# Three small moves in a transformer kernel: conv weights halved on GpSimd, bias copies moved into the feed-forward part, selector and factor tiles of the head norms widened to 128 partitions

## The chip, the cores and the metric

One core of a Trainium2 chip runs the whole kernel. A core has TensorE (PE, with its weight loads in rows of their own, PEld), VectorE (DVE), ScalarE (ACT), GpSimd (POOL) and the queues that start transfers (SP's, ACT's and POOL's). The metric is the device time in microseconds; several runs are given, and one more execution was profiled.

## The reference

Two blocks on 256 tokens of width 1024, in fp32. The first is a hybrid layer (dilated attention beside a state-space scan, then a gated feed-forward part). The second has two layers that work on a context stream `c` and an image stream `x` of 256 tokens each. In each: a modulated norm and a feed-forward part, a mixing part, and a second feed-forward part. The mixing part of the first of these layers normalizes each head of its queries and keys; that of the second has latent attention, and a neighbourhood attention with a relative bias. Cut to what the change touches:

```python
def causal_depthwise_conv(x, w, bias):        # block 1: four taps a channel, then silu
...
def rms_norm(x, gain=None):                   # used per head: x is (B, S, heads, 64)
    y = xf * lax.rsqrt(jnp.mean(xf * xf, axis=-1, keepdims=True) + EPS)
...
    aq = apply_rope2d(rms_norm(aq.reshape(B, S, A_HEADS, HEAD_DIM), a_q_norm), *rope)
    ak = apply_rope2d(rms_norm(ak.reshape(B, S, A_KV_HEADS, HEAD_DIM), a_k_norm), *rope)
...
        bias = rpb_f[:, dr_idx[None, :, None], dc_idx[:, None, :]]   # neighbourhood attention
        s = jnp.einsum('bqhd,bjkhd->bhqjk', q_row, k_band).astype(jnp.float32) * scale + bias
```

## The kernel before

**Products.** Activations lie transposed, features on partitions and tokens in the free dimension. Each fp32 product is made of three matmuls in the type fp32r: `wh` by the high part of the activations (L139), `wh` by their low part (L140), `wl` by the high part (L141). A weight slab of 128 x 1024 (512 KB) is loaded by SP's queue into one of five `wraw` buffers (L113); ACT makes `wh` of it by a cast (L120), DVE makes `wl` by a subtraction (L121). A slab feeds 24 matmuls of 256 or 512 columns. In the first block and on `x` alone the moving side has 256 columns; where `c` and `x` are taken side by side it has 512.

**Order.** `K.run` issues units (one column of 128 outputs each) and pieces of other work between them: `weave` spreads a list of steps over a list of units, and `later` puts a step off until the next product has been issued, so that PE has work while other engines prepare. A scheduler then orders the instructions of each engine by priority.

**Head norms.** `HeadNorm` belongs to the mixing parts `mix_ab` and `mix_cd`. For each block of 128 outputs (two heads of 64, or a head's 64 with 32 rotary rows) ACT copies and squares the product (`add`). A matmul with a block of ones gives the heads' sums of squares with tokens on partitions (L1047, two columns). DVE turns them into 1/rms. Two transposes (L1056) bring these factors back to one row per head, and `K.split` writes their high part into rows 0 to n-1 and their low part into rows 32 to 32+n-1 of a tile `rh` (`self.r`, one of a ring of four), the other rows being zero. Then, for each block, L1071 multiplies a selector `sel` by `rh`, which spreads each head's factor over the partitions of that head in PSUM, and DVE multiplies the block by it (L1073, or L1077 to L1081 with rotary tables). L1071 stands between matmuls of the products, one at a time or in pairs.

**Start of block 1.** `start` halves the taps and biases of the convolution (`cw`, L908), which are part of the constants `cols` that a DMA brings. DVE also sums squares for the first norm (`acc`, L322; PE sums them over partitions at L345), and copies the attention's bias rows out of PSUM (L507, after L506 on PE). POOL's queue writes these rows out (L508) and loads them back as bias tiles (L527).

**Neighbourhood bias.** `rpb` is a DRAM tile with 64 copies of the bias (8 heads x 889), so that `mix_cd` can read it with a skew (`load_bias`, on SP's queue, with an addition on POOL at L1615). `bias_rows` makes 8 steps of 8 copies each, from DRAM to DRAM on POOL's queue (L1643). `block2` puts them among the 40 background pieces of the feed-forward part of its first layer; since they wait for nothing, the scheduler sets them early.

Of the kernel before, what the change touches and what calls it, by code (L numbers as in the profile page):

```python
# [8 lines left out]
F32 = mybir.dt.float32  # L9
F32R = mybir.dt.float32r  # L10
AF = mybir.ActivationFunctionType
ALU = mybir.AluOpType
# [4 lines left out]
T = 256  # L17
# [446 lines left out]
def block1(K, start_mod):  # L464
    nc, tc, A = K.nc, K.tc, K.A
# [14 lines left out]
    cw = xpool.tile([128, 128], F32, name="cw")[:, :120]  # L480
    K.gap(xpool, 320)
    K.gap(xpool, 352)
    at, _ = COLS["conv_w"]
# [421 lines left out]
    sctx, qctx, yctx = ExitStack(), ExitStack(), ExitStack()  # L905

    def start():
        nc.vector.tensor_scalar(cw, K.cols[:, at:at + 120], 0.5, None, op0=ALU.mult)  # L908

    def heads_done():  # L910
        hctx.close()
# [28 lines left out]

    scan0 = scan(0)
    items = weave(qkv_units(0), [bias_row(0), start, bias_row(1), lambda: load_bias(0), bias_row(2)], 3, 2)
    items += weave(qkv_units(1) + [dt_unit] + b_units, attention(0) + [lambda: load_bias(1)])
    items += weave(qkv_units(2) + c_units + x_units(0), attention(1) + [lambda: load_bias(2)])
# [21 lines left out]
    fctx = ExitStack()  # L966
    K.gap(K.pool(fctx, "gap1", 1), 192)
    hid_p = K.pool(fctx, "b1h", 14)

    def c_square(b):  # L970
        return lambda: K.square_add("c", K.X["c"][:, b], b == 0)

    steps = K.pieces(16) + [c_square(b) for b in range(KB)]
# [114 lines left out]
def head_selectors(K, pool, width, rows, n):  # L1088

    nc, A = K.nc, K.A  # L1090
    at, n2 = COLS[f"sum{width}"]
    sums = K.cols[:rows, at:at + n2]
    raw = K.raw_p.tile([128, 1024], F32, name="wraw")
    sel = pool.tile([48, n * 128], F32R, name=f"sel{width}")
    nc.scalar.dma_start(raw[:48, :n * 128], A[f"sel{width}"])
    nc.vector.tensor_copy(sel, raw[:48, :n * 128])
    return sums, sel


def stacked(K, pool):  # L1100

    zero = K.t1("zero")
    K.nc.vector.memset(zero, 0.0)
    ring = []
    for i in range(4):
        ring.append(pool.tile([48, T], F32R, name=f"rh{i}"))
        K.nc.scalar.copy(ring[i], zero[:48])
    return ring


# [63 lines left out]
def out_proj(K, src, layer, streams, done, steps=()):  # L1174
    def evac(m):
        return lambda s, p: K.residual(s, m, p, K.mod(layer, s, 5)(m), True)

    K.run(weave([K.lin(src, m, K.acts, evac(m)) for m in range(KB)], steps), streams, done=done)


def mix_ab(K, streams):
# [14 lines left out]
    rctx = ExitStack()  # L1196
    rp = K.pool(rctx, "abr", 1)
    s64, sel64 = head_selectors(K, rp, 64, 128, 5)
    ring = stacked(K, rp)
    cos, sin = K.t1("cos"), K.t1("sin")  # L1200
    nc.scalar.dma_start(cos, A["rope_cos"])
# [209 lines left out]
def mix_cd(K, streams):  # L1411
# [28 lines left out]
    tctx = ExitStack()  # L1440
    tp = K.pool(tctx, "cdt", 1)
    s64, sel64 = head_selectors(K, tp, 64, 128, 5)
    s96, sel96 = head_selectors(K, tp, 96, 96, 4)
    ring = stacked(K, tp)

    rank = {("q", "x"): 6, ("k", "x"): 2, ("k", "c"): 2}
# [189 lines left out]
    ctx.close()  # L1636


def bias_rows(K):

    K.rpb = K.dram.tile([64, 8, 7 * 127], F32, name="rpb")
    rows = K.A["rpb"][:, 4:11].rearrange("h r c -> h (r c)").unsqueeze(0).to_broadcast([8, 8, 7 * 127])
    return [lambda i=i: K.nc.gpsimd.dma_start(K.rpb[8 * i:8 * i + 8], rows) for i in range(8)]  # L1643


def block2(K, layers=(0, 1)):
    nc, A = K.nc, K.A
    for layer in layers:
        both = ["c", "x"]

        def norms(i, layer=layer):
            return lambda s: K.norm_stream(s, K.mod(layer, s, i + 1), K.mod(layer, s, i))

        steps = K.pieces(40)
        if layer == 0:
            steps[10:10] = bias_rows(K)
        fctx = ExitStack()
        hid_p = K.pool(fctx, "h1", 14)
        K.ffn(A[f"f1g{layer}"], A[f"f1u{layer}"], [A[f"f1d{layer}{i}"] for i in range(3)], both,
              lambda s, m: K.mod(layer, s, 2)(m), hid_p, steps, norms(3))  # L1660
        fctx.close()
        K.dbg(f"d_xf{layer}", K.X["x"])
        K.dbg(f"d_cf{layer}", K.X["c"])
        if layer == 0:
            mix_ab(K, both)
            out_proj(K, A["ab_out"], 0, both, norms(6))
            tail = both
        else:
            while K.bg:
                K.background()  # L1670
            K.mctx.close()
            mix_cd(K, both)
            out_proj(K, A["cd_out"], 1, ["x"], norms(6))
            tail = ["x"]
        K.dbg(f"d_xm{layer}", K.X["x"])
        K.dbg(f"d_cm{layer}", K.X["c"])
        fctx = ExitStack()
        if layer == 1:
            K.gap(K.pool(fctx, "gap2", 1), 192)
        hid_p = K.pool(fctx, "h2", 14)  # L1680

        def done(s):
            K.norm_stream(s, K.mod(1, s, 1), K.mod(1, s, 0))

        def after(s, m):
            if layer == 1:
                nc.sync.dma_start(A["out"][:, m], K.X["x"][:, m])

        K.ffn(A[f"f2g{layer}"], A[f"f2u{layer}"], [A[f"f2d{layer}{i}"] for i in range(3)], tail,
              lambda s, m: K.mod(layer, s, 8)(m), hid_p, K.pieces(40 if layer == 0 else 0),  # L1690
              done if layer == 0 else None, after)
        fctx.close()
        K.dbg(f"d_x2{layer}", K.X["x"])
# [62 lines left out]
def constants():  # L1756
    import numpy as np
    f = np.float32
    c = {}
    i = np.arange(128)  # L1760
    c["ident"] = np.eye(128, dtype=f)
    c["tri"] = (i[:, None] <= i[None, :]).astype(f)
    for g, d in ((1, 4), (2, 16)):
        seg = T // d
        ok = (i[:, None] // seg == i[None, :] // seg) & (i[:, None] >= i[None, :])
        c[f"mask{g}"] = np.where(ok, 0.0, NEG).astype(f)

    def bucket(dist):
        dist = np.asarray(dist)
        big = 16 + (np.log(np.maximum(dist, 1).astype(f) / f(16)) / f(math.log(2048 / 16)) * f(16)).astype(np.int32)  # L1770
        return np.where(dist < 16, dist, np.minimum(big, 31))

    oh = np.zeros((33, 896), f)
    for g, (c0, n, off, d) in enumerate(((0, 383, 255, 1), (384, 255, 127, 4), (640, 255, 127, 16))):
        u = np.arange(n)
        oh[np.where((off - u >= 0) & (off - u <= 128), bucket(np.clip(off - u, 0, 128) * d), 32), c0 + u] = 1.0
    c["onehot"] = oh
    sel = np.zeros((8, 512), f)
    for h in range(8):
        sel[h, h * 64:h * 64 + 64] = 1.0  # L1780
    c["sel"] = sel
    for name, rows, n in (("sel64", [64, 64], 5), ("sel96", [64, 32], 4)):
        sel = np.zeros((48, n, 128), f)
        for b in range(n):
            at = 0
            for e, r in enumerate(rows[:2]):
                sel[[2 * b + e, 32 + 2 * b + e], b, at:at + r] = 1.0
                at += r
        c[name] = sel.reshape(48, n * 128)
    t = np.arange(T)  # L1790

    def rope(dim):
        nf = dim // 4
        inv = (f(10000.0) ** (-np.arange(nf, dtype=f) / f(nf))).astype(f)
        ang = np.concatenate([(t // 64).astype(f)[:, None] * inv, (t % 64).astype(f)[:, None] * inv], axis=-1)
        cos, sin = np.cos(ang.astype(np.float64)).astype(f), np.sin(ang.astype(np.float64)).astype(f)
        full = lambda a, sign: np.stack([sign * a.reshape(T, 2, nf), a.reshape(T, 2, nf)], axis=2).reshape(T, dim).T
        return full(cos, 1), full(sin, -1)

    cos, sin = rope(64)  # L1800
    c["rope_cos"], c["rope_sin"] = np.tile(cos, (2, 1)), np.tile(sin, (2, 1))
    cos, sin = rope(32)
    c["mla_cos"] = np.concatenate([np.ones((64, T), f), cos])
    c["mla_sin"] = np.concatenate([np.zeros((64, T), f), sin])
    q, k = i[:, None], i[None, :]
    c["amask"] = np.stack([np.where(k + 128 - q <= 128, 0.0, NEG), np.where(q + 128 - k <= 128, 0.0, NEG)], 1).astype(f)
    cq = np.tile(np.arange(64), 2)[:, None]
    ck = np.tile(np.arange(64), 4)[None, :]
    start = np.clip(cq - 8, 0, 48)
    c["dmask"] = np.where((ck >= start) & (ck < start + 16), 0.0, NEG).astype(f)  # L1810
    return {k: np.ascontiguousarray(v, dtype=f) for k, v in c.items()}


def prepare(inp):
    import numpy as np
    f = np.float32
    I = {k: np.asarray(v) for k, v in inp.items()}
    out = constants()
    feat = lambda a: np.ascontiguousarray(a.reshape(T, KB, 128).transpose(2, 1, 0))
    out["x"], out["ctx"] = feat(I["x"][0]), feat(I["ctx_2"][0])  # L1820
# [101 lines left out]
```

## Time and profile before

| | |
|---|---|
| Time of three runs | 2482.21, 2473.56, 2483.57 us, median 2482.21 |
| Time of the profiled execution | 2473.19 us |
| Its span, first to last instruction | 2471.4 us |
| PE busy | 2415.3 us, 98% |
| PEld (weight loads, beside PE) | 2101.6 us, 85% |
| DVE, ACT, POOL busy | 1642.8, 1064.7, 34.3 us |
| Mean granted TensorE clock | 0.985 |

PE is busy nearly all the time in every stage but the first microseconds. "Busy" says only that PE had a matmul in it: how fast these follow each other is read from their starts. The profiled execution took 1.8 us more than its span, and 9.0 us less than the median of the three runs.

### The profile page before, as it was taken

The page shows a single profiled execution, that of the slowest core. Times are in us where ns is not written, and L with a number is a line of the kernel's source. Part 1 is how long each engine was busy: PE and PEld are TensorE (multiplying, and loading weights), DVE is VectorE, ACT ScalarE, POOL GpSimd, SP SyncE. Part 2 cuts the span into 40 slices and gives each one's busy share as a digit, 9 for nine tenths or more (in the row PEclk, how much of TensorE's full clock was granted, in tenths as well). Part 3 has the DMA queues.
Part 4 walks back from the last instruction along what each step waited for, and adds up shares of the span by engine and source line. Part 5 has one row for each costly group of instructions (what it writes and reads, how often), then busy time and mean ns, then how long its engine had stood idle before and what let it go on. Part 6 is the DMA issues. An engine that isn't in the chain of part 4 may idle for free.

```text
span 2471.4 us, 38395 instructions
## 1 busy us (share of the span) xinstructions
PE 2415.3 (98%) x15104; PEld 2101.6 (85%) x15104; DVE 1642.8 (66%) x3016; ACT 1064.7 (43%) x1934; POOL 34.3 (1%) x56
## 2 busy tenths in 40 slices
PE   7999999999999999999999999999999999999999
PEld 6998999999988888886498888888888888876999
DVE  5767787787865666778757666656555555667655
ACT  4566565535632222535743222243222234555443
POOL 3000000000000000000000000000000000000000
PEclk9999899999999999999899999999999999999999
DMA  9455455676454554341014555534555422233554
GB/s 271 153 154 157 134 175 174 212 251 225 148 177 136 170 173 144 112 139 52 1 52 154 165 159 162 165 108 142 180 166 171 150 87 84 100 97 86 169 195 133
DMA packets 113157, 363.38 MB, mean 147 GB/s; under 512 B 21186, under 2 KB 23562, under 8 KB 112976
## 3 DMA queue, kind: packets, MB, share of 16 engines
q1 hardware_dynamic: 109232, 352.58, 45.1%
q0 software_dynamic: 2176, 5.09, 0.9%
q10 hardware_dynamic: 1568, 3.25, 0.4%
q8 instruction: 119, 1.95, 0.3%
q14 instruction: 62, 0.51, 0.1%
HBM read 359.33 MB, written 3.36 MB: 147 GB/s over the span
## 4 chain that ended last, share of the span: by engine, by line
PE 70%; DVE 3%; ACT 2%; issue 1%; DMA 0%; ACTq 0%; DVEq 0%
PE pm L139 20%; PE pm L140 20%; PE pm L141 20%; PE pt L1140 1%; PE pa L1047 1%; PE pm L1339 1%; PE pt L1071 1%; PE pa L1592 1%; DVE wl L121 1%; PE pm L1600 1%; PE pa L1355 1%; PE pm L1279 1%; PE pa L1316 0%; PE pm L1622 0%; PE pm L1165 0%
## 5 line engine op out<-in xcount | busy, mean ns | idle before, releaser
L139 PE MATMUL pm<-ah,wh 128*128 128x256 f32 (+2 forms) x3096 | 1002.9, 326 | 13.1 <-ACT ah L370 10.7
L140 PE MATMUL pm<-al,wh 128*128 128x256 f32 (+2 forms) x3096 | 997.4, 323 | 1.1 <-DVE al L371 1.0
L141 PE MATMUL pm<-ah,wl 128*128 128x256 f32 (+2 forms) x3096 | 996.1, 322 | 0.0
L120 ACT CAST wh<-wraw 128x1024 fp32r<-128x1024 f32 (+4 forms) x535 | 541.0, 1014 | 946.0 <-PE pm L140 750.3
L121 DVE TENSOR_TENSOR wl<-wraw,wh 128x1024 fp32r<-128x1024 f32 (+4 forms) x535 | 627.5, 1176 | 228.3 <-ACT wh L120 225.8
L139 PEld LDWEIGHTS pm<-ah,wh 128*128 128x128 f32 (+1 forms) x3096 | 590.1, 192 | 67.8 <-ACT ah L370 12.3
L140 PEld LDWEIGHTS pm<-al,wh 128*128 128x128 f32 (+1 forms) x3096 | 591.9, 191 | 49.0 <-issue 2.7
L141 PEld LDWEIGHTS pm<-ah,wl 128*128 128x128 f32 (+1 forms) x3096 | 592.2, 191 | 46.6 <-issue 2.3
L140 PE MATMUL pm<-hl,wh 128*128 128x512 f32 (+1 forms) x934 | 312.6, 335 | 0.0
L139 PE MATMUL pm<-hh,wh 128*128 128x512 f32 (+1 forms) x934 | 312.1, 334 | 0.0
L141 PE MATMUL pm<-hh,wl 128*128 128x512 f32 (+1 forms) x934 | 312.1, 334 | 0.0
L1001 DVE SCALAR_TENSOR_TENSOR junk<-wraw,cactc 128x1024 f32<-128x1024 f32 x112 | 137.2, 1225 | 183.1 <-DMA wraw<-w_mod 183.0
L1001 DVE SCALAR_TENSOR_TENSOR junk<-wraw,cactx 128x1024 f32<-128x1024 f32 x144 | 176.1, 1223 | 48.8 <-DMA wraw<-w_mod 46.2
L139 PEld LDWEIGHTS pm<-hh,wh 128*128 128x128 f32 x934 | 175.7, 188 | 18.7
L140 PEld LDWEIGHTS pm<-hl,wh 128*128 128x128 f32 x934 | 175.7, 188 | 18.6
L141 PEld LDWEIGHTS pm<-hh,wl 128*128 128x128 f32 x934 | 175.8, 188 | 18.4
L125 ACT CAST hh<-g 128x512 fp32r<-128x512 f32 (+1 forms) x113 | 59.1, 525 | 228.4 <-DVE g L428 228.4
L428 DVE TENSOR_TENSOR g<-g,pm 128x512 f32<-128x512 f32 (+1 forms) x113 | 64.0, 567 | 55.6 <-PE pm L141 54.1
L126 DVE TENSOR_TENSOR hl<-g,hh 128x512 fp32r<-128x512 f32 (+1 forms) x113 | 63.9, 567 | 0.3
L458 DVE SCALAR_TENSOR_TENSOR xc<-pm,mcol0c,xc 128x256 f32<-128x256 f32 x56 | 26.9, 481 | 53.5 <-PE pm L141 53.3
L424 ACT ACTIVATE g<-pm 128x512 f32<-128x512 f32 (+1 forms) x116 | 55.9, 486 | 2.0 <-PE pm L141 2.0
L1140 PEld LDWEIGHTS pt<-ident,e 128*128 128x128 f32 x272 | 30.7, 145 | 22.0 <-issue 18.6
(425 smaller groups left out, 2260.0 us busy)
## 6 DMA issues: line engine op xcount, KB each, us to landing
wraw<-w_mod SPq DMA_DIRECT2D x144, 512.0 KB, 4.0
wraw<-f1g SPq DMA_DIRECT2D x44, 512.0 KB, 3.9
wraw<-f1u SPq DMA_DIRECT2D x44, 512.0 KB, 4.2
wraw<-f2g SPq DMA_DIRECT2D x44, 512.0 KB, 3.6
wraw<-f2u SPq DMA_DIRECT2D x44, 512.0 KB, 3.6
wraw<-f1d SPq DMA_DIRECT2D x32, 512.0 KB, 3.9
wraw<-f2d SPq DMA_DIRECT2D x32, 512.0 KB, 3.6
wraw<-w_xbc SPq DMA_DIRECT2D x24, 512.0 KB, 3.7
```

The source lines that it names most:

```text
L120: nc.scalar.copy(h[:, :f], raw[:, :f])
L121: nc.vector.tensor_tensor(lo[:, :f], raw[:, :f], h[:, :f].bitcast(F32), op=ALU.subtract)
L125: self.nc.scalar.copy(h, src)
L126: self.nc.vector.tensor_tensor(lo, src, h.bitcast(F32), op=ALU.subtract)
L139: nc.tensor.matmul(out, h[:, c], ah, start=first, stop=False)
L140: nc.tensor.matmul(out, h[:, c], al, start=False, stop=False)
L141: nc.tensor.matmul(out, lo[:, c], ah, start=False, stop=last)
L424: nc.scalar.activation(half(g["g"], s), p, AF.Silu)
L428: nc.vector.tensor_tensor(t, t, p, op=ALU.mult)
L458: self.nc.vector.scalar_tensor_tensor(x, p, gate, x, op0=ALU.mult, op1=ALU.add)
L1001: nc.vector.scalar_tensor_tensor(junk, raw, 1.0, K.cact[s], op0=ALU.mult, op1=ALU.mult, accum_out=K.mcol[layer, s][:, j:j + 1])
L1140: nc.tensor.transpose(p[:, j * 128:(j + 1) * 128], b, K.ident)
```

## The change

Three parts. `cw` is halved on POOL in place of DVE (L908). `sel` and the four tiles of the ring have 128 partitions in place of 48 (the selector's constant, its load, its cast and the ring's zeroing with them), so L1071 contracts over 128 rows, of which the new ones are zero. And `bias_rows` first loads the 8 x 889 bias into an SBUF tile `rpbrow` of the feed-forward part's pool `h1`, then writes the 64 copies from there; the pool is opened ahead of it.

```diff
@@ mix1: start
-        nc.vector.tensor_scalar(cw, K.cols[:, at:at + 120], 0.5, None, op0=ALU.mult)
+        nc.gpsimd.tensor_scalar(cw, K.cols[:, at:at + 120], 0.5, None, op0=ALU.mult)
@@ head_selectors
-    sel = pool.tile([48, n * 128], F32R, name=f"sel{width}")
-    nc.scalar.dma_start(raw[:48, :n * 128], A[f"sel{width}"])
-    nc.vector.tensor_copy(sel, raw[:48, :n * 128])
+    sel = pool.tile([128, n * 128], F32R, name=f"sel{width}")
+    nc.scalar.dma_start(raw[:, :n * 128], A[f"sel{width}"])
+    nc.vector.tensor_copy(sel, raw[:, :n * 128])
@@ stacked
-        ring.append(pool.tile([48, T], F32R, name=f"rh{i}"))
-        K.nc.scalar.copy(ring[i], zero[:48])
+        ring.append(pool.tile([128, T], F32R, name=f"rh{i}"))
+        K.nc.scalar.copy(ring[i], zero)
@@ bias_rows
-def bias_rows(K):
+def bias_rows(K, pool):
     K.rpb = K.dram.tile([64, 8, 7 * 127], F32, name="rpb")
-    rows = K.A["rpb"][:, 4:11].rearrange("h r c -> h (r c)").unsqueeze(0).to_broadcast([8, 8, 7 * 127])
-    return [lambda i=i: K.nc.gpsimd.dma_start(K.rpb[8 * i:8 * i + 8], rows) for i in range(8)]
+    rows = pool.tile([8, 896], F32, name="rpbrow", bufs=1)[:, :7 * 127]
+    copies = rows.unsqueeze(1).to_broadcast([8, 8, 7 * 127])
+    steps = [lambda: K.nc.gpsimd.dma_start(rows, K.A["rpb"][:, 4:11].rearrange("h r c -> h (r c)"))]
+    return steps + [lambda i=i: K.nc.gpsimd.dma_start(K.rpb[8 * i:8 * i + 8].rearrange("q h u -> h q u"), copies)
+                    for i in range(8)]
@@ block2
         steps = K.pieces(40)
         if layer == 0:
-            steps[10:10] = bias_rows(K)
-        fctx = ExitStack()
-        hid_p = K.pool(fctx, "h1", 14)
+            steps[10:10] = bias_rows(K, hid_p)
@@ constants
-        sel = np.zeros((48, n, 128), f)
+        sel = np.zeros((128, n, 128), f)
```

DVE at the start of the program, where `acc` holds the sums of squares and `ct` the bias rows:

```order
 L898 MEMSET half 128x1
 L965 MEMSET one 128x1
-L908 TENSOR_SCALAR cw<-cols 128x120
 L322 TENSOR_TENSOR acc<-acc,sq 128x256 x2
 L507 COPY ct<-pa 8x384
```

The sums that stood behind L908 on DVE are now behind nothing but their squares. On POOL, L908 stands ahead of the first write of the bias rows (L508) in the place of the first copy of `rpb`. The other copies stood on POOL's queue as follows (`bias` are the attention's bias tiles, `xc` the rotary tables of `mix_cd`):

```order
 L527 DMA bias_1434<-brow_109 16x8x128 x8
 L527 DMA bias_2308<-brow_110 16x8x128 x8
-L1643 DMA rpb<-rpb 64x1x889 x7
+L1644 DMA rpbrow<-rpb 8x889
+L1645 DMA rpb<-rpbrow 8x8x889 x8
 L1419 DMA xc<-mla_cos 96x256
```

The place in POOL's row is the same, but the load now waits: its tile lies where block 1's feed-forward part had its hidden activations, so it starts when PE has read the last of those (about 650 us in the trace of before), and the copies start behind it.

The scheduler also moved a few instructions in block 1. PE of before, among the products of unit `pm_779`, where L581 gives attention scores of the second pair of heads:

```order
L141 MATMUL pm_779<-ah1_213,wl_665 128x256
L139 MATMUL pm_779<-ah1_213,wh_664 128x256
L140 MATMUL pm_779<-al1_214,wh_664 128x256
L141 MATMUL pm_779<-ah1_213,wl_665 128x256
L581 MATMUL pa_753<-k_359,q_326 128x128
L581 MATMUL pa_753<-k_359,q_326 128x256
```

And PE of the change there (`pm_726` is the unit ahead of it):

```order
L141 MATMUL pm_726<-ah1_213,wl_627 128x256
L139 MATMUL pm_779<-ah1_213,wh_664 128x256
L140 MATMUL pm_779<-al1_214,wh_664 128x256
L141 MATMUL pm_779<-ah1_213,wl_665 128x256
L139 MATMUL pm_779<-ah1_213,wh_664 128x256
L140 MATMUL pm_779<-al1_214,wh_664 128x256
L141 MATMUL pm_779<-ah1_213,wl_665 128x256
L581 MATMUL pa_753<-k_359,q_326 128x128
L581 MATMUL pa_753<-k_359,q_326 128x256
```

The scores stand behind two triples of the unit in place of six, 12 matmuls earlier. On ACT and DVE the instructions around this pair change places accordingly (the exponentials L598, a cast or subtraction of weights). Elsewhere PE's order is the same, L1071 and its neighbours included.

## Rows read from the trace of the kernel before

**Rows 1.** Page, part 1: busy time of PE.

```profile
PE 2415.3 (98%) x15104; PEld 2101.6 (85%) x15104; DVE 1642.8 (66%) x3016; ACT 1064.7 (43%) x1934; POOL 34.3 (1%) x56
```

**Rows 2.** Windows: us, busy by engine (instructions), granted clock, DMA share, GB/s.

```profile
40.00:60.00 20.00, 19.96 (x173) 19.76 (x172) 9.68 (x10) 8.88 (x14) 7.10 (x13) 1.00 1.04 295
240.00:260.00 20.00, 20.00 (x62) 14.40 (x61) 9.30 (x25) 3.25 (x8) 0.00 (x0) 0.50 0.19 64
660.00:680.00 20.00, 19.42 (x118) 17.35 (x119) 16.98 (x33) 8.74 (x15) 0.00 (x0) 1.00 0.35 110
1050.00:1140.00 90.00, 89.86 (x489) 75.48 (x488) 65.71 (x180) 28.42 (x67) 0.00 (x0) 1.00 0.36 115
2100.00:2190.00 90.00, 90.00 (x619) 76.97 (x618) 60.58 (x160) 41.51 (x101) 0.00 (x0) 1.00 0.34 112
```

**Rows 3.** Instructions of L1071: ns least/median/most, first and last start, forms.

```profile
L1071 PE MATMUL pt<-rh,sel x64: 276/356/384, 1077.4 to 2187.3; 48*128 48x256 f32 x38, 48*64 48x256 f32 x16, 48*96 48x256 f32 x10
```

**Rows 4.** Timeline of PE, single L1071: start, duration, operation.

```profile
2128.00 0.28 PE L140 MATMUL pm<-lq,wh 128*96 128x256 f32 x1
2128.12 0.28 PE L141 MATMUL pm<-hq,wl 128*96 128x256 f32 x1
2128.33 0.38 PE L1071 MATMUL pt<-rh,sel 48*128 48x256 f32 x1
2128.64 0.36 PE L139 MATMUL pm<-hq,wh 128*96 128x256 f32 x1
2128.83 0.28 PE L140 MATMUL pm<-lq,wh 128*96 128x256 f32 x1
```

**Rows 5.** Timeline of PE, a pair of L1071 among products of 512 columns.

```profile
1084.30 0.50 PE L1071 MATMUL pt<-rh,sel 48*128 48x256 f32 x2
1084.73 0.50 PE L139 MATMUL pm<-ah,wh 128*128 128x512 f32 x1
1085.07 0.40 PE L140 MATMUL pm<-al,wh 128*128 128x512 f32 x1
1085.31 0.40 PE L141 MATMUL pm<-ah,wl 128*128 128x512 f32 x1
```

**Rows 6.** Timeline of PE, an L1071 of 64 output columns.

```profile
2132.51 0.33 PE L1071 MATMUL pt<-rh,sel 48*64 48x256 f32 x1
2132.77 0.36 PE L140 MATMUL pm<-lq,wh 128*96 128x256 f32 x1
2132.97 0.28 PE L141 MATMUL pm<-hq,wl 128*96 128x256 f32 x1
```

**Rows 7.** Timeline of PE, matmuls of 128 rows and 64 columns in block 1.

```profile
82.51 0.88 PE L618 MATMUL pm<-pts,vt 128*64 128x128 f32 x12
83.31 0.39 PE L139 MATMUL pm<-ah,wh 128*128 128x256 f32 x1
83.53 0.28 PE L140 MATMUL pm<-al,wh 128*128 128x256 f32 x1
```

**Rows 8.** Waits of DVE, 2085 to 2190 us: what for, us in total, times, longest.

```profile
DVE vc L1073 <- PE pt L1071: 5.5, 1, 5.5
```

**Rows 9.** Timeline of DVE and PE at the start; brackets: idle before, and its releaser.

```profile
9.19 0.22 DVE L908 TENSOR_SCALAR cw<-cols 128x120 f32<-128x120 f32 x1 [7.78 <-DMA cols<-cols]
9.33 0.95 DVE L322 TENSOR_TENSOR acc<-acc,sq 128x256 f32<-128x256 f32 x2
15.59 1.02 PE L345 MATMUL pt<-ones,acc 128*128 128x1 f32 x4 [3.78 <-DVE acc L322]
```

**Rows 10.** Instructions of L1615, POOL's nearest operation to L908.

```profile
L1615 POOL TENSOR_TENSOR bias<-bias,dmask x8: 1265/1272/1295, 2192.9 to 2239.1; 128x512 f32<-128x512 f32 x8
```

**Rows 11.** Instructions of L1643, all eight.

```profile
L1643 POOL DMA_DIRECT2D rpb<-rpb x8: 554/557/601, 4.1 to 53.5; - x8
```

**Rows 12.** Timeline of SP's queue around 660 us: weight loads.

```profile
658.23 0.33 SPq L113 DMA_DIRECT2D wraw<-f1u  x1
671.49 0.33 SPq L113 DMA_DIRECT2D wraw<-w_mod  x1
```

More of the change, by code (lines that the diff above doesn't have):

```diff
@@ L1652, in norms @@
             return lambda s: K.norm_stream(s, K.mod(layer, s, i + 1), K.mod(layer, s, i))
+        fctx = ExitStack()
+        hid_p = K.pool(fctx, "h1", 14)
         steps = K.pieces(40)
         if layer == 0:
-            steps[10:10] = bias_rows(K)
-        fctx = ExitStack()
-        hid_p = K.pool(fctx, "h1", 14)
+            steps[10:10] = bias_rows(K, hid_p)
         K.ffn(A[f"f1g{layer}"], A[f"f1u{layer}"], [A[f"f1d{layer}{i}"] for i in range(3)], both,
@@ L1788, in constants @@
                 at += r
-        c[name] = sel.reshape(48, n * 128)
+        c[name] = sel.reshape(128, n * 128)
     t = np.arange(T)
```

## Prediction

> **What bounds the kernel now.** I read the page's part 1 first: PE is busy 98% of the span, DVE 66% [rows 1]. So a gain must come out of PE's own time, or out of the few gaps that PE has. Then the windows of the two stretches in which L1071 runs [rows 2, 3]: PE is busy 89.86 of 90 us in the one and 90.00 of 90 in the other, at a granted clock of 1.00, with DVE at 65.7 and 60.6 us and the DMA share at 0.36 and 0.34. There PE ends last, and every wait of DVE for an L1071 (5.5 us for one of them [rows 8]) is a wait for PE's queue. But busy is not fast. The last view is PE's timeline, by the starts: a product's matmul of 256 columns follows the one before it by 0.12 us (2128.00 to 2128.12), and that pitch breaks round each L1071 [rows 4].
>
> **The selector matmuls.** From 2128.12 (L141) to 2128.83 (the second product behind L1071) are three steps that would take 3 x 0.12 = 0.36 us at the pitch of the products; they take 0.71 [rows 4]. The surplus is 0.35 us: L1071 starts 0.09 late, holds PE for 0.31 in place of 0.12, and the product behind it is followed 0.07 late. For a pair, 1084.30 to 1085.07 is 0.77, where two matmuls of 256 columns and one of 512 would take 0.24 + 0.24 (1085.07 to 1085.31): surplus 0.29 us [rows 5]. The moving side is 256 columns and the type the same as in the products, and the output has 128 or 96 columns as theirs has. What differs is that L1071 stands on 48 rows of the array and they on 128. I take it that PE empties when the row shape changes, both ways, and that an L1071 of 128 rows runs at the pitch of its neighbours. Of the 64 instructions 38 have 128 output columns and 10 have 96 [rows 3]; by the timeline 32 of these 48 stand alone among products, 14 in seven pairs, and two beside other narrow matmuls, which I count at nothing. The gain is 32 x 0.35 + 7 x 0.29 = 11.2 + 2.0 = 13.2 us.
>
> The 16 with 64 output columns still differ from the products after the change, in columns. Matmuls of 128 rows and 64 columns are in the trace: the product behind L618 is followed by the next after 0.22 in place of 0.12 us [rows 7], so the break is there with full rows too. I take no gain for these 16. The upper bound is their present surplus: 2132.51 to 2132.97 is 0.46 against 0.24, and 0.09 ahead of it as for the others: 0.31 us, 16 x 0.31 = 5.0 us [rows 4, 6]. The lower bound for the 48 uses the same rows the other way: if a late product behind a foreign matmul has nothing to do with rows [rows 7], 32 + 7 times about 0.08 us, 3.1, stay, and the gain is 10.1. DVE doesn't take the gain away: 65.7 us of work in a stretch that would be about 6 us shorter is 78% [rows 2].
>
> A rule of the Trainium skill speaks against this part. Its page "TensorE: Matmul & The Clock Gate", section "LDWEIGHTS (loading the stationary operand)", says: "A 32×128 weight load takes the same time as a 128×128 weight load", since only the columns count; the same page puts a single matmul of 32 rows at the time of one of 128. By it alone the widening is worth 0 and the sum is the start's gain below. The trace agrees that weights aren't what is long; it doesn't agree that a matmul of 48 rows among 128-row products costs the same, 0.71 against 0.36 us [rows 4].
>
> **The start.** L908 stands on DVE until 9.19 us for the constants, and two sums of squares behind it start at 9.33 and take 0.95; the last sum releases PE at 15.59, after a wait of 3.78 us [rows 9]. Without L908 these two can run while DVE stood idle, and what is behind them moves forward. Bounds 0 (another input ends last) and 0.95 + 0.22, the two sums and L908 itself; I take 0.4 us, near the middle, because the bias-row copies between the sums wait for PE's first matmuls. On POOL the halving costs between its 0.22 on DVE and 1.27, the nearest operation there [rows 9, 10]; behind it stand the writes of the bias rows, which wait for DVE's copies behind the same sums anyway. `cw` is first used by the convolution's units, which stand behind the first units of queries, keys and values. If that cover were gone, the bias tiles would come up to about 1 us late.
>
> **The copies of the neighbourhood bias.** Eight POOL-queue transfers leave the time to 53.5 us [rows 11]. PE is busy 19.96 of 20 us there with the DMA share at 1.04 [rows 2], so the relief is worth nothing. They come back around 655 to 680 us, where the DMA share is 0.35 [rows 2]; SP issues one weight load in 13 us there [rows 12], so there are buffers ahead. Nothing but the mixing part of the last layer reads the copies, 1,500 us later [rows 10]. I take 0; the upper price is a rival below. The eight copies now start from 8 partitions of SBUF, which no row here prices.
>
> **The rest.** The selector's load and cast and the ring's zeroing keep their counts, and lie beside full PE. The scores moved 12 matmuls forward (about 1.4 us) ask for their inputs earlier: 0 if they are there, at most that 1.4 us lost; I take 0, since DVE and ACT work in the same order on them.
>
> **Sum.** 13.2 + 0.4 = 13.6 us less. From the profiled execution, 2473.2, that gives 2459.6. But that execution is among the lower ones: it and the three runs are 2473.2, 2473.6, 2482.2 and 2483.6, mean 2478.1. The changed kernel will be seen in the same spread, so I put the point at 2478.1 - 13.6 = 2464.5 us. A change under 0.5%, 12.4 us, can hardly be told from none here.
>
> **Rivals.**
> (a) The row count isn't what breaks the pitch; any matmul of another kind between the products does. For: behind L618 with its 128 rows the break is there [rows 7]. Against: L1071 itself, of the same type and moving width as its neighbours, holds PE for 0.31. Time: only the start's 0.4 is gained, 2473 to 2483. The skill's rule above leads to this case. Chance 0.18.
> (b) Half of it: the break behind and ahead stays (0.16 each time, 39 x 0.16 = 6.2), L1071's own 0.19 goes: gain about 7 us, 2466 to 2476. Chance 0.15.
> (c) The 16 narrow ones gain too: 13.6 + 5.0 = 18.6, 2454.6 from the profiled execution, 2459.5 from the mean. Chance 0.14.
> (d) Slower: the copies from 8 partitions, 1.8 MB in all, hold the engines' queues so that weight loads of the feed-forward part at 655 to 690 us come late. For: in that stretch PE already lost 0.58 of 20 us to waits, so it runs near its supply [rows 2]. Against: 13 us between loads [rows 12]. Each microsecond of delay beyond the buffers' lead is lost; with half of those 13 us as the lead, about 7, it cancels the gain from 20 us on, and the kernel is 0.5% slower from 33 us on. Chance 0.05, three in five of it beyond that. A granted clock of half in a further stretch would do the same: between 240 and 260 us PE made 62 instructions at 0.50, where 40 to 60 has 173 at 1.00; such 20 us cost at least 10 [rows 2]. Chance 0.03, as the places of these stretches aren't explained.
>
> **Chances.** My forecast (10 to 15 us less) holds the remaining 0.45. It lies close to the bound of 12.4, so I count two thirds of it, 0.30, and all of (c), 0.14, as faster, and a little of (b) and (a), 0.06, for the spread between runs; faster 0.50. Slower 0.05 (most of (d), and a little of the spread on (a)). The rest, 0.45, is within 0.5%. The range reaches from (c) off the lower base, 2454, less a microsecond for its bounds, to (a) at the mean, 2478, with 1 us for the scores: 2453 to 2479. It leaves out the upper half of (a) and (d). The forecast's own range is 2458 to 2472.
>
> **What the changed profile would show.** In PE's timeline round 2128 L1071 as 128*128 with starts 0.12 apart, no late start ahead or behind; the times between first and last L1047 in each of the two stretches about 6 us shorter; the 64-column ones as before. DVE's first L322 before 9 us, and L345 about 0.4 ahead of 15.59. The transfer of `rpbrow` near 650 us, weight loads behind it landing as now, and PE's waits between 650 and 690 no longer. A surplus of 0.35 still there round L1071 makes (a) right, one of 0.16 (b); a new wait of PE for `wh` at 660 to 690 makes (d) right. What would make the prediction wrong without any of these is a half-clock stretch that comes or goes, about 10 us a time.

## The result and the profile after

The changed kernel took 2458.53 us, the median of five runs (2455.92 to 2466.05), against 2482.21 of five runs of the kernel before (2473.56 to 2484.38). The ratio is 0.9919, with a 95% interval of 0.9893 to 0.9945, about 20 us less (the medians alone are 23.7 apart). The profiled execution took 2460.47 us (span 2458.6), which is 12.7 us less than the profiled execution of before, 2473.19. The five runs of before spread over 11 us and its profiled execution lies at their low end, which is part of why the two differences are apart.

PE's busy time, in the first part of the page, fell by 13.8 us, and DVE's hardly [rows 1]:

```profile
PE 2401.5 (98%) x15104; PEld 2101.4 (85%) x15104; DVE 1641.2 (67%) x3015; ACT 1063.9 (43%) x1934; POOL 35.4 (1%) x58
```

The instructions of L1071 in the changed kernel: least, median and most ns, first and last start, forms (beside [rows 3]):

```profile
L1071 PE MATMUL pt<-rh,sel x64: 276/282/392, 1080.3 to 2173.3; 128*128 128x256 f32 x38, 128*64 128x256 f32 x16, 128*96 128x256 f32 x10
```

The median fell from 356 to 282 ns, but the better figure is in the starts: from the first L1071 to the last it is 1093.0 us, where before it was 1109.9. Between them stand the same products, so the selector matmuls gave some 17 us. That difference still holds what the two profiles differ by in stretches at half the clock. In the two stretches in which L1071 stands, about 1075 to 1141 and 2099 to 2190 us, the clock is at 1.00 in both, and there the same matmuls gain 6.5 and 11.2 us by their starts, 17.6 in all. Yet the first comes 2.9 us later than before (1077.4): something ahead of it lost time.

PE's timeline of the changed kernel in the second stretch, start and duration:

```profile
2122.77 0.28 PE L141 MATMUL pm<-hq,wl 128*96 128x256 f32 x1
2122.89 0.28 PE L1071 MATMUL pt<-rh,sel 128*128 128x256 f32 x1
2123.01 0.28 PE L139 MATMUL pm<-hq,wh 128*96 128x256 f32 x1
...
2125.45 0.28 PE L139 MATMUL pm<-hq,wh 128*96 128x256 f32 x1
2125.56 0.28 PE L1071 MATMUL pt<-rh,sel 128*64 128x256 f32 x1
2125.68 0.28 PE L140 MATMUL pm<-lq,wh 128*96 128x256 f32 x1
2125.80 0.28 PE L141 MATMUL pm<-hq,wl 128*96 128x256 f32 x1
```

L1071 starts 0.12 us behind its neighbour and is followed 0.12 later, with 128 output columns and with 64 alike [rows 4, 6].

At the start (DVE and PE; in brackets the idle time before and what ended it) the sums of squares no longer wait for the constants, and PE's L345 comes 0.27 us earlier [rows 9]:

```profile
6.40 0.96 DVE L322 TENSOR_TENSOR acc<-acc,sq 128x256 f32<-128x256 f32 x2 [5.01 <-ACT sq L321]
15.32 1.02 PE L345 MATMUL pt<-ones,acc 128*128 128x1 f32 x4 [3.78 <-DVE acc L322]
```

And here is what was lost. The windows of the changed kernel behind the new copies (us; PE, PEld, DVE, ACT and POOL busy; granted clock; DMA share; GB/s):

```profile
660.00:680.00 20.00, 20.00 (x115) 18.22 (x116) 10.50 (x21) 7.28 (x12) 0.00 (x0) 0.91 0.95 56
...
720.00:740.00 20.00, 18.72 (x82) 15.14 (x82) 18.13 (x28) 8.07 (x11) 0.00 (x0) 1.00 0.71 229
```

From 660 to 680 the DMA engines are busy 95% of the time and move 56 GB/s, where they were busy 35% at 110 before [rows 2]. The weight loads issued from 655 to 690 us (L113) landed so, first before, then in the changed kernel:

```profile
DMA to landing us min/median/max: 3.5/4.3/5.1
```

```profile
DMA to landing us min/median/max: 13.2/18.0/31.5
```

DVE has 10.50 us of work from 660 to 680 in place of 16.98, since the weights that it should take up haven't come. Its longest wait from 650 to 700 us (in total, times, longest; before it was 3.4, 4 times, at most 1.3):

```profile
DVE junk L1001 <- DMA wraw<-w_mod: 15.9, 2, 15.1
```

It does that work later, and PE then waits for it, for the gated activations `g` of the feed-forward part. The longest wait of PE from 655 to 760 us, at 724 to 726:

```profile
PE pm L139 <- DVE g L428: 1.3, 1, 1.3
```

That wait isn't there before, where PE's longest from 640 to 760 us is 1.0 us, for ACT's `ah`, which the changed kernel has too. By the starts of the same matmuls PE lost 3.3 us between 640 and 745 us against before: 1.3 in the wait for `g`, and about 1.7 in a stretch of 3.4 us at half the clock at 660 us. The eight copies, issued from 650.6 us on, took this long to land (before, from DRAM, the median was 9.0):

```profile
DMA to landing us min/median/max: 11.0/22.4/33.1
```

### The profile page after: what moved, and what is told of

It reads as the page before. It is cut to its first block, busy times and chain, and to the rows that moved or that the text cites. A ratio compares the mean times of both kernels' runs of the same rounds, so it can differ in the third digit from the quotient of the medians.

```text
span 2458.6 us, 38408 instructions
## 1 busy us (share of the span) xinstructions
PE 2401.5 (98%) x15104; PEld 2101.4 (85%) x15104; DVE 1641.2 (67%) x3015; ACT 1063.9 (43%) x1934; POOL 35.4 (1%) x58
## 4 chain that ended last, share of the span: by engine, by line
PE 68%; DVE 3%; ACT 2%; DMA 2%; issue 1%; DVEq 0%; ACTq 0%
PE pm L139 20%; PE pm L140 19%; PE pm L141 19%; DMA wraw<-w_mod 2%; PE pt L1140 1%; PE pa L1047 1%; DVE wl L121 1%; PE pm L1339 1%; PE pa L1592 1%; PE pm L1600 1%; PE pa L1355 1%; PE pm L1279 1%; PE pa L1316 0%; DVE junk L1001 0%; PE pt L1071 0%
## 5 line engine op out<-in xcount | busy, mean ns | idle before, releaser
L322 DVE TENSOR_TENSOR acc<-acc,sq 128x256 f32<-128x256 f32 x105 | 42.2, 418 | 13.1 <-ACT sq L321 12.9
```

Source lines behind the costliest of these rows:

```text
L322: nc.vector.tensor_tensor(self.acc[key], self.acc[key], sq, op=ALU.add)
```

## The experiments

Main theory: the 128 rows of L1071 make the whole gain; the move of L908 gives a few tenths; the copies from SBUF cost 1 to 4 us. Rivals: the gain lies in another part, the row count as such isn't what matters, the copies are hidden.

**e1_rows48**, one part undone:

```diff
-    sel = pool.tile([128, n * 128], F32R, name=f"sel{width}")
+    sel = pool.tile([48, n * 128], F32R, name=f"sel{width}")
...
-        ring.append(pool.tile([128, T], F32R, name=f"rh{i}"))
+        ring.append(pool.tile([48, T], F32R, name=f"rh{i}"))
...
```

> The changed kernel with sel and the ring back on 48 partitions; the other two parts stay. If the 128 rows of L1071 make the gain, as I hold: L1071 holds PE for 0.31 us again (0.26 with 64 columns) with late starts of 0.08 to 0.09 on either side, the stretches 1050 to 1140 and 2100 to 2190 are together 18 us longer than in the changed kernel, and the ratio to before is 0.998 to 1.003. If another part made it: stretches as in the changed kernel or a ratio near 0.992 all the same.

Measured: ratio to before 1.0012 (0.9994 to 1.003). Its L1071 instructions:

```profile
L1071 PE MATMUL pt<-rh,sel x64: 276/356/385, 1078.8 to 2186.7; 48*128 48x256 f32 x38, 48*64 48x256 f32 x16, 48*96 48x256 f32 x10
```

First to last is 1107.9 us, the median 356 ns. Without the rows the change gives nothing that the runs resolve.

**e2_rows128_only**, the same lines on 128 partitions in the kernel before, and nothing else:

```diff
-    sel = pool.tile([48, n * 128], F32R, name=f"sel{width}")
+    sel = pool.tile([128, n * 128], F32R, name=f"sel{width}")
...
```

> The kernel before with sel and the ring on 128 partitions and nothing else. If the rows make the gain: L1071 follows at 0.12 us, 18 us less in the two stretches, ratio 0.991 to 0.994, and weight loads behind 655 us land in about 4 us as before, with no wait of PE near 730 us. If the other parts are needed for it: ratio 0.997 or above.

Measured: ratio 0.994 (0.9915 to 0.9966).

```profile
L1071 PE MATMUL pt<-rh,sel x64: 276/282/392, 1079.5 to 2172.8; 128*128 128x256 f32 x38, 128*64 128x256 f32 x16, 128*96 128x256 f32 x10
```

First to last is 1093.3 us, as in the changed kernel, and PE has no wait for DVE's `g` between 640 and 760 us. The rows alone make the gain in the two stretches; the ratio, 0.6% against the changed kernel's 0.8%, isn't told apart from it. The scores of block 1 (L581) stand where they stood before in this kernel, and 12 matmuls earlier in e1_rows48, e4_cw_dve and e10_late_dram: that shift came with the late copies and not with the tiles.

**e3_bias_dram**, the copies as before the change:

```diff
-            steps[10:10] = bias_rows(K, hid_p)
+            steps[10:10] = bias_rows(K)
...
```

> The changed kernel with the eight copies of the bias from DRAM to DRAM again, set early as before. If the copies from SBUF at 650 to 690 us cost something there (weight loads late, DVE's work put off, PE waiting 1.3 us for it near 730 us): that wait is gone, PE gains 1 to 3 us between 655 and 745 us over the changed kernel, and between 40 and 60 us loses about 0.6 of it. If they are hidden: no difference in either place, and the time within 0.2% of the changed kernel's.

Measured: 2455.0 us, ratio 0.9921 (0.9895 to 0.9948), which the changed kernel's interval doesn't tell apart. In the profile the wait for `g` is gone and the DMA share from 650 to 690 us falls back to 0.46, against 0.94 in the changed kernel (first the changed kernel, then this one):

```profile
650.00:690.00 40.00, 38.46 (x225) 34.31 (x225) 18.32 (x42) 12.31 (x22) 4.50 (x8) 0.96 0.94 113
```

```profile
650.00:690.00 40.00, 37.79 (x232) 33.57 (x231) 32.94 (x65) 17.76 (x30) 0.00 (x0) 1.00 0.46 143
```

DVE has 32.94 us of work in this stretch, the changed kernel 18.32. By the starts of the same matmuls PE gains 3.3 us between 655 and 745 us over the changed kernel, a little over the 1 to 3 expected; about half of it is the half-clock stretch at 660 us, which is gone too. From 22 to 100 us it loses 0.3, but there the edit isn't the copies alone: the scores of block 1 stand 70 matmuls later on PE. The copies aren't hidden, and what they cost is under what the runs resolve.

**e4_cw_dve**, L908 back on DVE:

```diff
-        nc.gpsimd.tensor_scalar(cw, K.cols[:, at:at + 120], 0.5, None, op0=ALU.mult)
+        nc.vector.tensor_scalar(cw, K.cols[:, at:at + 120], 0.5, None, op0=ALU.mult)
```

> The changed kernel with L908 back on DVE. I expect L322 to start at 9.3 us again, the first product 0.25 to 0.4 us later than in the changed kernel, and nothing else: the time within 0.2% of it, ratio to before about 0.992. The rival, that the halving on POOL delays the bias rows and costs as much as it gives, would show the same first product and DVE waiting less for bias tiles near 62 us.

Measured: ratio 0.995 (0.9931 to 0.9968), 2462.75 us. L322 starts at 9.33 again:

```profile
9.33 0.95 DVE L322 TENSOR_TENSOR acc<-acc,sq 128x256 f32<-128x256 f32 x2
```

The first product starts at 20.30 us. Over all profiles it starts at 20.30 to 20.40 with L908 on DVE (three kernels) and at 19.70 to 20.06 with L908 on POOL (ten). So this part gives 0.25 to 0.7 us at the first product.

The ratio is further from the changed kernel's than that, by 0.003, and over the 0.2% expected, though the intervals overlap. The profiled execution is 17.7 us longer in span than the changed kernel's. By the starts of the same matmuls, 2.4 of them come between 30 and 60 us, where PE waits 1.2 us for ACT (L553 for L545), which the changed kernel doesn't; some 5 at half-clock stretches at 291 and 325 us (the changed kernel has as much half clock in all, at other places); and 6 from a slower pitch in the last feed-forward part (last section). Whether L908 is behind the 2.4 isn't told by one profile: e2_rows128_only, with L908 on DVE and early copies, doesn't lose them. The two kernels with 128 rows and L908 on DVE lie at 0.994 and 0.995, the three with it on POOL and 8-row combine weights at 0.992. So I don't read the 0.003 as the price of L908, but the runs don't exclude that part of it is.

**e5_rows64** and **e6_rows96**, other row counts in the lines of e1_rows48 (64 and 96 for 48):

> The changed kernel with sel and the ring on 64 partitions. If the break in the pitch comes from a row shape of the array of which there are few sizes, and 48 rows are placed in one of 64: 64 rows cost what 48 did, L1071 starts 0.09 us late, holds PE for 0.31 and the next product is followed 0.08 late, and the two stretches are 18 us longer than in the changed kernel. If unused rows within a shape cost time: 64 rows, with none unused, run at 0.12 us.

> The changed kernel with sel and the ring on 96 partitions. If the row shape is what counts and 96 rows are placed in one of 128: L1071 runs at 0.12 us with no late starts, the stretches as in the changed kernel. If every count below that of the neighbours breaks the pitch: 0.31 us and late starts, 18 us more in the two stretches.

```profile
L1071 PE MATMUL pt<-rh,sel x64: 276/356/384, 1085.0 to 2195.1; 64*128 64x256 f32 x38, 64*64 64x256 f32 x16, 64*96 64x256 f32 x10
```

```profile
L1071 PE MATMUL pt<-rh,sel x64: 278/284/388, 1078.8 to 2171.8; 96*128 96x256 f32 x38, 96*64 96x256 f32 x16, 96*96 96x256 f32 x10
```

The first is e5_rows64, the second e6_rows96; each was run once (2481.50 and 2458.65 us). With 64 rows it is 1110.1 us from first to last and a median of 356 ns, as with 48. With 96 it is 1093.0 and 284, as with 128. By the starts of the same matmuls the two stretches of L1071 are 17.4 us shorter than before with 96 rows, 17.6 in each kernel that has 128 rows in fp32r, and 0.0 with 64. So unused rows cost next to nothing. What costs is a row shape other than that of the neighbours; as far as these four counts tell, 96 rows share the shape of 128 while 64 and 48 share another.

**e7_comb128**, the same edit at another place, block 1's combine weights, which stand on 8 rows among products of 128:

```diff
-        comb["sel"] = ssd["gts"][:8, 0:2].rearrange("p a t -> p (a t)")
+        comb["sel"] = ssd["gts"][:, 0:2].rearrange("p a t -> p (a t)")
+        comb["wide"] = ssd["ub"][:, 0:3]
+        nc.gpsimd.memset(comb["wide"], 0.0)
...
-            nc.tensor.matmul(p[:, :T], comb["sel"][:, b * 128:(b + 1) * 128], comb["rm"][:, g], start=True, stop=True)
+            nc.tensor.matmul(p[:, :T], comb["sel"][:, b * 128:(b + 1) * 128], comb["wide"][:, g], start=True, stop=True)
...
```

> The changed kernel with the combine weights of block 1 (L669, 12 matmuls on 8 rows between 236 and 255 us) spread over 128 rows too, the new ones zero (a selector of 128 x 512 and a POOL memset). If a break costs 0.2 to 0.35 us here as it did at L1071: 2 to 4 us less around 240 us. If besides the matmuls on 8 rows are why the granted clock falls to half there for 20 to 24 us: that stretch at half the clock is gone, and about 10 us more is won. If the clock falls for another reason: it falls all the same, at the same place.

Measured: 2447.17 us, ratio 0.9896 (0.9859 to 0.9933). The window from 235 to 265 us, first in the changed kernel, then in this one:

```profile
235.00:265.00 30.00, 28.94 (x127) 23.55 (x127) 18.41 (x42) 9.13 (x20) 0.00 (x0) 0.66 0.18 54
```

```profile
235.00:265.00 30.00, 28.36 (x238) 26.55 (x238) 29.05 (x60) 15.92 (x31) 0.00 (x0) 1.00 0.42 126
```

The clock stays at 1.00 and PE makes 238 instructions in place of 127; by the starts of the same matmuls, 11.3 us are won between 230 and 270 us. The changed kernel has 20.5 us at half the clock there, which cost 9 to 10 of them (its products follow each other by 0.21 us in place of 0.12). That leaves 1 to 2.5 us for the breaks themselves, at the lower end of the 2 to 4 expected or below it; L669 is fp32, and the product behind it is still followed late (239.22 to 239.52 us). The interval of the ratio overlaps with the changed kernel's; the gain is read from the profiles.

**e8_fp32**, L1071 with 128 rows, read as fp32:

```diff
-            nc.tensor.matmul(r, self.sel[:, cs], self.r, start=True, stop=True)
+            nc.tensor.matmul(r, self.sel[:, cs].bitcast(F32), self.r.bitcast(F32), start=True, stop=True)
```

> The changed kernel with L1071 read as fp32 in place of fp32r, 128 rows as before: tells why a product behind L618 (128 rows, 64 columns) is followed late although an L1071 of 64 columns no longer is. If the type is what breaks the pitch there: L1071 takes about 0.43 us and the second product behind it comes 0.08 to 0.1 late again, some 20 to 25 us more in the two stretches. If it is the output's columns or the short moving side of L618: L1071 takes longer, but the products behind it follow at 0.12.

Each L1071 is now two instructions. PE's timeline:

```profile
2126.42 0.28 PE L139 MATMUL pm<-hq,wh 128*96 128x256 f32 x1
2126.54 0.62 PE L1071 MATMUL pt<-rh,sel 128*128 128x256 f32 x2
2126.80 0.47 PE L140 MATMUL pm<-lq,wh 128*96 128x256 f32 x1
2127.11 0.28 PE L141 MATMUL pm<-hq,wl 128*96 128x256 f32 x1
```

There is no late start ahead (0.12 us), the pair takes 0.26, less than the 0.43 that I expected, and the product behind it is followed after 0.31 in place of 0.12. So the type alone, with the second instruction that it brings, makes the product behind late, with full rows and full columns. The one run took 2482.60 us, and by the starts the two stretches are 22.9 us longer than in the changed kernel, as the first case expected (20 to 25).

**e9_best**, the two edits of e3_bias_dram and e7_comb128 together:

> The changed kernel with the two edits that looked better than it: the bias copies from DRAM as before the change (early), and the combine weights L669 on 128 rows. If the copies from SBUF cost 1.3 to 3.6 us and the half-clock stretch near 240 us hangs on the matmuls of 8 rows: no wait of PE for DVE's g between 680 and 740 us, no half clock between 235 and 265 us, and about 12 us less than the changed kernel, ratio to before 0.985 to 0.989. If the clock in the last such run was chance: the stretch of 17 to 24 us is back and the ratio is 0.990 to 0.993.

Measured: 2450.81 us, ratio 0.9895 (0.9865 to 0.9925); in the profile a granted clock of 1.00 from 235 to 265 us and no wait for `g`. That is 7.7 us under the changed kernel's median, where about 12 and a ratio of 0.985 to 0.989 were expected. The ratio is no better than that of e7_comb128: its profiled execution shows two other half-clock stretches of 6.8 us each at 279 and 313 us, where e7_comb128 has one of 3.4 at 278.

**e10_late_dram**, the copies at the late time, but from DRAM:

```diff
+    src = K.dram.tile([8, 7 * 127], F32, name="rpb1")
-    copies = rows.unsqueeze(1).to_broadcast([8, 8, 7 * 127])
+    copies = src.unsqueeze(0).to_broadcast([8, 8, 7 * 127])
...
+             lambda: K.nc.gpsimd.dma_start(src, rows)]
...
```

> The changed kernel with the eight copies at the same late time, but read from a row in DRAM (rpbrow is written there first) and not from 8 partitions of SBUF. If the slow source is what delays the weight loads: the copies land in about 8 to 11 us each as the early ones did, the stretch with a DMA share near 0.95 is under 15 us in place of 33, and PE doesn't wait for DVE's g between 680 and 740 us. If the time is the cause, 1.8 MB at 655 us whatever the source: PE waits 1.3 us or more there again.

Measured: ratio 0.9922 (0.9893 to 0.9951). PE has no wait for `g` between 640 and 760 us. The copies landed so:

```profile
DMA to landing us min/median/max: 3.4/6.4/9.7
```

They carry the same bytes some 6 us later (from 656.8 us on), in 6.4 us in place of 22.4, and the DMA share from 650 to 690 us is 0.58. So the time isn't the cause. What is left is the way from 8 partitions of SBUF: the source, and with it the order in which the rows are written, which changed in the same edit and wasn't tried apart.

**e11_comb64**, the edit of e7_comb128 on 64 rows:

> The changed kernel with the combine weights L669 on 64 rows. By the row shape as seen at L1071 these still break the pitch on both sides (late start, late second product), where 128 rows didn't. If the half clock near 240 us comes with the broken pitch, a stretch of 17 us or more at half the clock is there; if it comes with few rows, it is shorter than with 8 rows or gone.

One run of 2454.73 us. The granted clock from 235 to 265 us:

```profile
235.00:265.00 30.00, 28.64 (x177) 23.73 (x178) 24.04 (x52) 12.40 (x25) 0.00 (x0) 0.89 0.30 87
```

There is one half-clock stretch of 6.8 us, shorter than with 8 rows in most profiles (17 to 24 us), and longer than with 128 (none). The expectation spoke of 17 us or more if the half clock came with the broken pitch; but e8_fp32, with 8 rows, has only 6.8 us too, so this run doesn't decide between its two cases.

## Why the prediction was right, and what it mis-sized

The sign, the place and the mechanism were right; the size was short. That the profiled difference, 12.7 us, lies near the 13.6 of the sum is luck: the 16 narrow matmuls gave about 5 more than foretold, and the copies and the clock took about as much away.

**The selector matmuls.** The 48 matmuls with 128 and 96 columns gave what was worked out for them: the starts round them are now 0.12 apart. The step that failed is "I take no gain for these 16": the ones with 64 columns run at 0.12 as well, so their whole surplus came back. That was rival (c): 13.2 + 5.0 = 18.2 us. From the last matmul ahead of each L1071 or pair to the second behind it, added up, the profiles show 13.2 us less for the 48 and 4.8 for the 16; by the stretches it is 17.6. The sign set for it, about 6 us less between first and last L1047 of each stretch, came out at 3.3 and 10.2: the narrow ones stand in the second, and in the first the last L1071 come behind the last L1047. The error was in reading [rows 7]. I put the late product behind L618 down to its columns. e8_fp32 shows a late product behind a matmul of full rows and columns that is read as fp32, and the 64-column L1071 shows that narrow columns in fp32r leave none. L618's operands are fp32 by the code, so the type is enough to explain its late product; its shorter moving side and its alternating halves of the output weren't tried apart. Rival (a) is refuted by e1_rows48 and e2_rows128_only, where nothing but the rows differs, and (b) by the starts, 0.12 apart ahead and behind. e5_rows64 and e6_rows96 add that it is the row shape and not unused rows.

The rule of the Trainium skill that spoke against this part ("TensorE: Matmul & The Clock Gate", section "LDWEIGHTS (loading the stationary operand)") would have given no gain; the measurement decides against using it for a matmul that stands among others of another shape. The page "TensorEngine Tiling (Array Packing)", section "Key Properties", says that a change of tiling mode drains the engine. The trace agrees as far as it goes: it shows a break of 0.35 us round one matmul of another row shape [rows 4], not the drain itself, and none for 64 columns on 128 rows.

**The start.** 0.4 us was foretold; 0.26 us is in the profile at the first product, 0.25 to 0.7 over all kernels. On POOL the halving took 0.51 us, within its bounds.

**The copies.** "I take 0" was wrong, though by little, and rival (d) had the mechanism, but neither its place nor its price. Landing took 22.4 us in place of 9; the weights came late, DVE's work was put off, and PE waited for it, not for `wh` at 660 to 690 us as (d) said, but some 40 us later for `g`: 1.3 us in the changed kernel, and 1.6 to 3.6 in six other kernels with these copies (e8_fp32 waits 3.2 us longer for ACT's `ah` instead). In before, e2_rows128_only, e3_bias_dram, e9_best and e10_late_dram there is none. By (d) a delay beyond about 7 us is lost one for one; the first weight load behind the copies landed in 31.5 us in place of 3.5, and PE lost 1.3 to 3.3, so there was far more lead than half of the 13 us between loads. The 0.58 us that (d) read as running near the supply [rows 2] were a wait for DVE's `al` (L371) behind a norm, not for weights. What the row of the DMA share at 0.35 didn't tell is that copies from eight partitions keep the engines 95% busy at 56 GB/s. That a half-clock stretch of 3.4 to 6.8 us stands at 655 to 695 us in five of the eight kernels with these copies, and in none without, fits, but it wasn't isolated.

**The clock.** The mean granted clock was 0.983 in the changed kernel's profile and 0.985 before. At half the level a stretch loses about half its length, so by this estimate the two lost 2458.6 x 0.017 = 41.8 and 2471.4 x 0.015 = 37.1 us: about 5 us of the profiled difference. -17.6 from the two stretches, -0.3 from the start and +1.3 from the wait for `g` make -16.6; with the clock's 5 about -12, where 12.7 was measured. The 2.9 us by which the first L1071 came later hold 1.7 of that clock beside the wait. The 20 us of the five runs hold more executions, and I take them with 17 us as agreeing within their interval (14 to 27).

**The moved scores** cost nothing that the starts show between 60 and 220 us.

What stays open: why the clock falls at these places. e7_comb128 and e9_best show that no half clock stands from 235 to 265 us when L669 has 128 rows, and with 8 rows all ten profiled kernels have one there, before included; e8_fp32, with 8 rows, has only 6.8 us, as e11_comb64 with 64. Whether it hangs on rows, or on the time that PE loses round these matmuls, isn't told apart.

## What to carry to other kernels

Read PE's starts, not its busy time: a matmul with few rows among full ones can cost nearly four times its own work (0.47 in place of 0.12 us), and zero rows up to the neighbours' shape take that back at no cost in weight loads that the rows show (PEld busy 2101.6 us before, 2101.4 after). Judge a transfer by its landing time and GB/s from the same kind of source, not by the free share of the queues: copies from eight partitions kept the engines 95% busy for 56 GB/s, where 110 had taken 35%. Where weights come late, look for the wait tens of microseconds behind, on the engine that had to catch up.

## What the runs showed that I had not expected

The combine weights of 8 rows: widening them gave more than the head norms' break would explain, since the clock no longer fell there (0.66 to 1.00 between 235 and 265 us), about 11 us in the profile for twelve matmuls.

And the same products had two pitches. In the last feed-forward part they follow each other by 113.3 ns in most executions, and by about 117.7 in the profiles of e2_rows128_only, e4_cw_dve and e8_fp32, at a granted clock of 1.00 in both. One window, from the changed kernel and from e4_cw_dve, whose order on PE is the same there:

```profile
2300.00:2320.00 20.00, 20.00 (x179) 20.00 (x179) 11.26 (x14) 10.36 (x16) 0.00 (x0) 1.00 0.62 190
```

```profile
2300.00:2320.00 20.00, 20.00 (x173) 20.00 (x172) 13.15 (x16) 10.07 (x15) 0.00 (x0) 1.00 0.75 236
```

Over the last 160 us this is some 6 us. What sets the pitch wasn't tried.
